# Four spans instead of three in the last output stage, and norm scales spread by a repeated stationary operand

## The chip, the cores and the metric

The kernel runs on one core of one Trainium2 chip. The metric is the device time of one execution in microseconds; the median of the runs counts. A core has five engines that work side by side, each through its own queue in order: TensorE (PE; its weight loads are listed apart as PEld), VectorE (DVE), ScalarE (ACT), GpSimd (POOL) and SyncE (SP, which here only issues DMAs). They wait for each other through semaphores.

## The reference

One inference step of a decoder trunk of two layers, for 1024 tokens of a prompt and 8 short sequences of 4 tokens: 1056 tokens of width 1024, all in fp32. Layer 0 is an RG-LRU block (causal convolution, gated linear recurrence), layer 1 an HGRN2 block (linear attention with gates and a matrix state). Cut to what matters here:

```python
def _rmsnorm(x, gain):
    xf = x.astype(jnp.float32)
    y = xf * lax.rsqrt(jnp.mean(xf * xf, axis=-1, keepdims=True) + EPS)
    return (y * gain.astype(jnp.float32)).astype(x.dtype)

def _hgrn_layer(x, g_norm, w_in, lb, o_gain, w_out, S0):
    xn = _rmsnorm(x, g_norm)
    ...
    y = (o.reshape(Bsz, T, INNER_B) * jax.nn.silu(gate)).astype(x.dtype)
    return x + y @ w_out, S_T.astype(x.dtype)

# _trunk: layer 0, layer 1, then
    return _rmsnorm(x, final_gain), jnp.stack(hs), jnp.stack(bufs), jnp.stack(Ss)
```

The outputs are the normalised tokens and the states of both layers. The change touches the end of layer 1, `x + y @ w_out` and the final norm, and the way in which every norm brings its scale to the data.

## The kernel before

**Layout.** Everything is kept transposed: the 1024 features of a token lie over 8 tiles of 128 partitions (`KD = 8`), the 1056 tokens (`TOK`) along the columns. A stage works on spans of tokens: three chunks of 352 columns (`CH`) in most stages, quarters of 264 in the products of layer 1.

**A product** in nearly full fp32 precision is three passes of the type fp32r (`mm3`, L262 to L264): each operand is split into a high and a low part, and high x high, high x low and low x high are added in one PSUM bank. Each of the three loads 128 stationary columns of weights and streams the tokens of the span. fp32 operands that are not split are used for small products; in the trace each of these shows as two passes.

**A norm** needs the sum of squares of each token, which lies over partitions. ScalarE squares the 8 tiles (`AF.Square`), VectorE or GpSimd adds the squares into one tile `acc`, and PE multiplies `acc` with a column of ones (`norm_sum`, L295 to L299): for every 128 tokens it yields a PSUM column whose partition is the token. ScalarE takes the root (L470, L1724), VectorE the reciprocal (L472, L1727), so that a tile `r` (`nr`) holds the scale of token 128*i + p in row p, column i. The scale must then lie along the columns and be the same in all partitions. For that, VectorE multiplies the unit matrix `ident` with each column of `r` into a row of diagonal matrices `dg` (L473 and L476; L1728 and L1732), and PE multiplies a tile of ones with it (L478, L1738): every partition of the result `bc` holds the scales of the span. In layer 0, `norm` (L460 to L479) does this six times, three times for the input and three times for the norm between the layers.

**The last output stage** begins when nearly all of `y @ w_out` is done: 5 of the 8 blocks of 128 features (`K1 = 5`) have been added to the residual `x2` before. The loop over `OUT` at L1761 takes the tokens in three spans of 512, 288 and 256. For each span it runs over the 8 output tiles `m`: 9 products (3 blocks by 3 passes) into a bank, an addition to the residual on VectorE (L1781), a square on ScalarE (L1783), and the square added on GpSimd (L1792). For the last span the squares of `m` from 4 on are not added but summed by PE directly, each as it comes, into one bank per 128 tokens. The span before is finished inside the next one: at `m = RM = 3` PE does its sums (`summed`) and the roots, at `m = SM = 6` its spread, followed by `finish` (L1747). `finish` scales the 8 tiles and sends them out: in the first span all 8 on VectorE (L1758, from PSUM); in later spans five there, and three by ScalarE (gain, L1755, possible earlier) and GpSimd (scale, L1756, from a copy of `bc` that ScalarE makes at L1751). The 8 output DMAs (recorded at L1759, issued by the helper at L332) alternate between the queues of SP and ScalarE. Behind the loop come two small products that keep PE busy (L1796), and the roots, spread and finishing of the last span.

**The order.** Within a layer the kernel does not issue instructions as it meets them: `fl.add` records each operation with its engine, an estimate of its duration, what it reads and writes and a priority, and at the end of the layer `fl.run` plans all of them (class `Flow`). The plan is a list schedule by priorities that are found from the far end backwards, followed by a random search over the operations of the first 60 us. PE operations marked `main=True` keep their order of recording; the others ("side") may go where the plan sees their inputs ready, with an extra distance `fl.side` from their producer (1.2 us by default, 0.4 in layer 1). The order of each engine is fixed by this before the kernel runs.

## Time and profile before

| | |
|---|---|
| median of 3 runs | 1031.57 us (1030.36 to 1032.78) |
| the profiled execution | 1031.86 us, of which the span of the profile is 1030.1 us |
| granted TensorE clock, mean | 0.997 of full speed |
| ACT, DVE and POOL busy in 981 to 998 us (first span) | 4.42, 5.39 and 7.03 us |
| the same in 1009.6 to 1019.4 us (third span) | 5.54, 8.52 and 4.88 us |
| output DMAs of 256, 144 and 128 KB, issue to landing | 1.7 to 2.6 us |

The span is what lies between the first and the last record; the time of a run has some more around it. A row of the timeline gives the start (us from the span's start), the time until the end, engine, line, operation, output and inputs, shapes, and the count where several like instructions follow each other (the duration is then that of all of them from the first start to the last end). A row of a group gives the line, engine, operation, shapes, the count, the busy time in us, the mean of one in ns, and the idle time before. A row of a stretch gives its bounds, its length and the busy us (with counts) of PE, PEld, DVE, ACT and POOL, then the granted clock, the share of the DMA engines and GB/s. Products are pipelined: a new one starts long before the record of the last ends, so that the pace of PE is read from start to start.

### The profile page before, as it was taken

To read this page: it belongs to the slowest core of one execution; us is meant where nothing else is said; L and a number is where in the kernel's file an instruction comes from. 1 tells how busy PE (TensorE), PEld (TensorE's weight loads), DVE (VectorE), ACT (ScalarE), POOL (GpSimd) and SP (SyncE) were. 2 spreads that over 40 slices of the span, in tenths; PEclk is the share of its full clock that TensorE was granted. 3 is DMA by queue.
4 is the path that set the end of the run, shared out by engine and by line. 5 is a ranking of instruction groups with operands and counts; after the bars stand their busy time and mean duration, and the time that the engine had idled before them with its cause. 6 is when DMAs were issued, how large, how long until landed. Compare 5 with 4: busy or idle time off the path is not lost.

```text
span 1030.1 us, 26451 instructions
## 1 busy us (share of the span) xinstructions
PE 1021.1 (99%) x10118; PEld 996.4 (97%) x10118; DVE 810.8 (79%) x1641; ACT 578.1 (56%) x1322; POOL 496.5 (48%) x569
## 2 busy tenths in 40 slices
PE   9999999999999999999999999999999999999997
PEld 9999999999999999999999999999999999999986
DVE  7999785867888699436599999798989799986436
ACT  8788747876775785335454463626363636552334
POOL 0117353544526236636425656555555557533544
PEclk9999999999999999999999999999999999999998
DMA  9201112112852487426474244343535353687204
GB/s 299 78 17 56 57 48 74 52 54 76 257 178 59 133 270 223 160 83 219 136 213 138 73 147 132 130 148 111 167 111 168 102 159 122 207 246 209 87 1 169
DMA packets 107854, 138.30 MB, mean 134 GB/s; under 512 B 23632, under 2 KB 85072, under 8 KB 107728
## 3 DMA queue, kind: packets, MB, share of 16 engines
q1 hardware_dynamic: 105424, 133.85, 42.1%
q10 hardware_dynamic: 2304, 2.77, 0.8%
q8 instruction: 79, 1.29, 0.5%
q14 instruction: 47, 0.39, 0.1%
HBM read 89.99 MB, written 41.61 MB: 128 GB/s over the span
## 4 chain that ended last, share of the span: by engine, by line
PE 93%; DVE 2%; DMA 2%; ACT 1%; issue 1%; POOL 1%; SPq 0%; POOLq 0%; DVEq 0%; ACTq 0%
PE mm L262 27%; PE mm L264 26%; PE mm L263 26%; PE hg L1085 2%; PE hg L592 1%; PE hg L262 1%; PE hg L264 1%; PE hg L263 1%; PE hg L753 1%; PE hg L1232 1%; PE hg L1287 1%; PE hg L1289 1%; DMA k<-yd 1%; PE mm L1085 0%; DMA vt<-sg 0%
## 5 line engine op out<-in xcount | busy, mean ns | idle before, releaser
L262 PE MATMUL mm<-xh,whi 128*128 128x352 f32 (+1 forms) x1127 | 352.6, 313 | 0.1
L264 PE MATMUL mm<-xh,wlo 128*128 128x352 f32 (+1 forms) x1127 | 348.1, 309 | 0.0
L263 PE MATMUL mm<-xl,whi 128*128 128x352 f32 (+1 forms) x1127 | 347.7, 309 | 0.0
L346 POOL TENSOR_TENSOR wlo<-wraw,whi 128x256 fp32r<-128x256 f32 (+3 forms) x188 | 200.8, 1084 | 199.7 <-ACT whi L403 97.3
L263 PEld LDWEIGHTS mm<-xl,whi 128*128 128x128 f32 x1127 | 212.5, 189 | 1.4 <-DVE xl L346 0.3
L262 PEld LDWEIGHTS mm<-xh,whi 128*128 128x128 f32 x1127 | 211.8, 188 | 2.1 <-DVE k L1545 0.3
L264 PEld LDWEIGHTS mm<-xh,wlo 128*128 128x128 f32 x1127 | 212.0, 188 | 0.0
L524 DVE SCALAR_TENSOR_TENSOR k<-xb,prm_sb,k 128x352 f32<-128x352 f32 (+2 forms) x144 | 82.3, 596 | 24.2 <-ACT k L521 20.7
L262 PE MATMUL mm<-t,whi 128*128 128x264 f32 (+1 forms) x330 | 96.6, 293 | 0.2 <-issue 0.2
L264 PE MATMUL mm<-t,wlo 128*128 128x264 f32 (+1 forms) x330 | 94.4, 286 | 0.0
L263 PE MATMUL mm<-t,whi 128*128 128x264 f32 (+1 forms) x330 | 94.4, 286 | 0.0
L1545 DVE TENSOR_TENSOR k<-mm,k 128x264 f32<-128x264 f32 x154 | 64.0, 424 | 11.7 <-PE mm L264 10.3
L346 POOL TENSOR_TENSOR wlo<-R,whi 128x256 fp32r<-128x256 f32 x70 | 58.3, 854 | 27.0 <-ACT whi L1469 24.1
L607 POOL TENSOR_TENSOR k<-X 128x352 f32<-128x352 f32 x36 | 43.6, 1217 | 52.8 <-DVE R L608 42.0
L1469 ACT CAST whi<-wraw 128x512 fp32r<-128x512 f32 x56 | 34.5, 618 | 60.4 <-DVE wraw L1479 26.0
L403 ACT CAST whi<-wraw 128x512 fp32r<-128x512 f32 (+2 forms) x79 | 44.3, 572 | 39.1 <-PE mm L263 28.9
L262 PEld LDWEIGHTS mm<-t,whi 128*128 128x128 f32 x330 | 62.1, 188 | 1.5 <-issue 0.3
L263 PEld LDWEIGHTS mm<-t,whi 128*128 128x128 f32 x330 | 62.2, 188 | 0.0
L264 PEld LDWEIGHTS mm<-t,wlo 128*128 128x128 f32 x330 | 62.1, 188 | 0.0
L262 PE MATMUL mm<-yh,whi 128*128 128x352 f32 x153 | 52.2, 341 | 0.0
L264 PE MATMUL mm<-yh,wlo 128*128 128x352 f32 x153 | 49.4, 323 | 0.0
L263 PE MATMUL mm<-yl,whi 128*128 128x352 f32 x153 | 49.4, 323 | 0.0
(458 smaller groups left out, 2513.9 us busy)
## 6 DMA issues: line engine op xcount, KB each, us to landing
wraw<-in_w_dram SPq DMA_DIRECT2D x88, 256.0 KB, 3.0
wraw<-in_wo_dram SPq DMA_DIRECT2D x34, 192.0 KB, 2.5
R<-in_w_dram SPq DMA_DIRECT2D x17, 256.0 KB, 3.9
si<-in_s_in_dram SPq DMA_DIRECT2D x8, 512.0 KB, 5.4
vt<-sg SPq DMA_DIRECT2D x8, 512.0 KB, 3.8
sg<-vt SPq DMA_DIRECT2D x32, 128.0 KB, 2.9
kt<-kt SPq DMA_DIRECT2D x8, 512.0 KB, 3.6
kt<-kt SPq DMA_DIRECT2D x32, 128.0 KB, 5.1
```

The lines of the kernel that those rows point to most:

```text
L262: T.matmul(out, wh, xh, start=first, stop=False)
L263: T.matmul(out, wh, xl, start=False, stop=False)
L264: T.matmul(out, wl, xh, start=False, stop=last)
L346: emit = lambda: e.tensor_tensor(b, x, a.bitcast(F32), op=ALU.subtract)
L403: act(m, lambda hi=hi, raw=raw, m=m: S.copy(hi[:, :m], raw[:, :m]), rk, (hk,), prio)
L524: dve(u, lambda src=src, dst=dst, sh=sh, k=k: V.scalar_tensor_tensor(dst, sh(src, k), pc("cw", 12 * k + m), dst, op0=ALU.mult, op1=ALU.add ...
L592: fl.add("PE", 0.62, lambda ps=ps, i=i, c=c: T.matmul(ps[:96, :CH], gs[:, i, :], ST[:96, chunk(c)], start=True, stop=True), (("gs",), *((" ...
L607: pool(CH, lambda x=x, a=a, b=b: G.tensor_tensor(x, a.bitcast(F32), b.bitcast(F32), op=ALU.add), (ak, bk), (xk,), 3)
L753: fl.add("PE", 0.25, lambda: T.matmul(warm[:, :128], ones, ones, start=True, stop=True), (), (wk,), 9)
L1085: T.matmul(ps[32 * j:32 * j + 32, n * w:n * w + w], B[:, o:o + 32], q(slice(o, o + 32)), start=True, stop=True, tile_position=(0, 32 * j))
L1469: act(512, lambda: S.copy(hi, raw), (rk,), (hk,), 2)
L1545: dve(QT, lambda: V.tensor_tensor(o[0], z[0], u[0], op=ALU.add), (z[1], u[1]), (o[1],), 0)
```

## The change

- `OUT` has four spans, of 448, 288, 192 and 128 tokens.
- The scales are spread without diagonal matrices. The new `spread_rows` multiplies, for each 128 tokens, column i of `r`, repeated 128 times as the stationary operand, with `ident`: row c of the unit matrix picks the scale of token c, and all 128 output partitions receive it. One fp32 product per 128 tokens takes the place of one product per span, and the VectorE operations that made `dg` go, in layer 1 and in the six norms of layer 0. There `dg` no longer takes a buffer of its ring.
- The sums and the spread of the span before are no longer `main` operations at `m = 3` and `m = 6`. They are recorded at `m = 0` as side operations and the plan places them, with `fl.side = 0.1` in this stage.
- In all spans but the last, the squares of `m = 6` and `m = 7` are added on VectorE instead of GpSimd.
- Estimates of the plan change with it (the spread's duration, the time that the output DMAs take), and `CUTS`, by which the residual's dependences are kept, follows the new spans.

```diff
--- before.py
+++ after.py
@@ -32,8 +32,7 @@
 SPOTS, SPOTS0, SPOTS1 = (-1, -1, 0, 2), (2, 5, -1, -1), (1, 5, 9, 13, 17, 20)
 K2 = 8 - K1
 NB4 = 6
-RM, SM = 3, 6
-OUT = ((0, 512), (512, 288), (800, 256))
+OUT = ((0, 448), (448, 288), (736, 192), (928, 128))
 
 D = 1024
 SEQ = 1024
@@ -298,6 +297,11 @@
         for s, (a, u) in zip(sums, spans(n)):
             T.matmul(s[:u], acc[:, a:a + u], ones[:, :1], start=start, stop=stop)
 
+    def spread_rows(bc, r, n):
+
+        for i, (a, u) in enumerate(spans(n)):
+            T.matmul(bc[:, a:a + u], r[:u, i:i + 1].to_broadcast([u, 128]), ident[:u, :u], start=True, stop=True)
+
     def new_acts():
         hs, ls = [], []
         for k in range(KD):
@@ -457,11 +461,10 @@
                 e = eng or G
                 (pool if e is G else dve)(CH, lambda: e.tensor_tensor(a[:, :CH], a[:, :CH], sq, op=ALU.add), (sk, ak), (ak,), 2)
 
-        def norm(acc, own=None, sums=None, sumk=()):
+        def norm(acc, sums=None, sumk=()):
 
             a, ak = acc
             r, rk = next(nrs)
-            dg, dk = own or next(xbs)
             if sums is None:
                 ps, pk = next(hg)
                 sums, sumk = [ps[:, i:i + 1] for i in range(4)], [pk]
@@ -470,12 +473,8 @@
                 act(4, lambda i=i, s=s, u=u: S.activation(r[:u, i:i + 1], s[:u], AF.Sqrt, bias=epsc[:u], scale=1.0 / D), sumk, (rk,), 0,
                     0.08)
             dve(4, lambda: V.reciprocal(r[:, :3], r[:, :3]), (rk,), (rk,), 0, True)
-            dve(256, lambda: V.tensor_tensor(dg[:, :256].rearrange("p (i n) -> p i n", i=2),
-                                             ident[:, None, :].to_broadcast([128, 2, 128]),
-                                             r[:, :2, None].to_broadcast([128, 2, 128]), op=ALU.mult), (rk,), (dk,), 0)
-            dve(96, lambda: V.tensor_scalar(dg[:, 256:CH], ident[:, :96], r[:, 2:3], None, op0=ALU.mult), (rk,), (dk,), 0)
             bc, bk = next(hg)
-            fl.add("PE", 0.7, lambda: T.matmul(bc[:, :CH], ones, dg[:, :CH], start=True, stop=True), (dk,), (bk,), 0)
+            fl.add("PE", 0.7, lambda: spread_rows(bc, r, CH), (rk,), (bk,), 0)
             return bc[:, :CH], bk
 
         def scaled_parts(c, k, x, xk, bc, bk, g, gk, e, prio=1):
@@ -894,7 +893,7 @@
                 squares(k, x, xk, accs[c], V, xos, (c, k) in MU)
             if c == 0:
                 dma(hct, hc, (), (("hct",),), 2, 196)
-            bc, bk = norm(accs[c], next(xrs))
+            bc, bk = norm(accs[c])
             if c == 0:
                 act(CH, lambda bc=bc: S.copy(bcs[0], bc), (bk,), (bcs[1],), 0)
             else:
@@ -1710,14 +1709,12 @@
                 key = ("spare", len(spare))
                 inherit(key, olds)
                 spare.append((o[:, a:a + 512], key))
-        accs, sqs, dgs, sb = cycle(spare[:2]), cycle(spare[2:5]), cycle(spare[5:7]), spare[7]
+        accs, sqs, sb = cycle(spare[:2]), cycle(spare[2:5]), spare[7]
         nr2 = cycle([(fixed(f"nr2{i}", [128, 4], F32, p1), ("nr2", i)) for i in range(2)])
 
         def roots(n, sums, ready):
 
             r, rk = next(nr2)
-            dg, dk = next(dgs)
-            f, u = n // 128, n % 128
             dve(4, lambda: V.memset(r, 1.0), (), (rk,), 0)
             srcs = [(slice(i, i + 1), s[:w]) for i, (s, (_, w)) in enumerate(zip(sums, spans(n)))]
             for q, src in srcs:
@@ -1725,23 +1722,18 @@
                     ready, (rk,), 0)
             w = len(srcs)
             dve(16, lambda: V.reciprocal(r[:, :w], r[:, :w]), (rk,), (rk,), 0)
-            dve(128 * f, lambda: V.tensor_tensor(dg[:, :128 * f].rearrange("p (i n) -> p i n", i=f),
-                                                 ident[:, None, :].to_broadcast([128, f, 128]),
-                                                 r[:, :f, None].to_broadcast([128, f, 128]), op=ALU.mult), (rk,), (dk,), 0)
-            if u:
-                dve(u, lambda: V.tensor_scalar(dg[:, 128 * f:n], ident[:, :u], r[:, f:f + 1], None, op0=ALU.mult), (rk,), (dk,), 0)
-            return dg[:, :n], dk
-
-        def spread(n, dg, dk, main):
+            return r, rk
+
+        def spread(n, r, rk, main):
 
             bc, bk = next(hg)
-            fl.add("PE", 0.002 * n, lambda: T.matmul(bc[:, :n], ones, dg, start=True, stop=True), (dk,), (bk,), 0, main=main)
+            fl.add("PE", 0.0023 * n, lambda: spread_rows(bc, r, n), (rk,), (bk,), 0, main=main)
             return bc[:, :n], bk
 
         def summed(acc, ak, n):
             s, sk = next(hg)
             sums = [s[:, i:i + 1] for i in range(4)]
-            fl.add("PE", 0.7, lambda: norm_sum(sums, acc, n, True, True), (ak,), (sk,), 0, main=True)
+            fl.add("PE", 0.7, lambda: norm_sum(sums, acc, n, True, True), (ak,), (sk,), 0)
             return roots(n, sums, (sk,))
 
         def finish(a, n, bc, bk):
@@ -1756,18 +1748,18 @@
                     pool(n, lambda x=x: G.tensor_tensor(x, x, sb[0][:, :n], op=ALU.mult), (sb[1], *xk), xk, 1)
                 else:
                     dve(n, lambda x=x, k=k: V.scalar_tensor_tensor(x, x, pc("gf", k), bc, op0=ALU.mult, op1=ALU.mult), (bk, *xk), xk, 1)
-                dma(yT[k][:, q], x, xk, (), 1, n / 2, S if k % 2 else Q)
-
+                dma(yT[k][:, q], x, xk, (), 1, 0.37 * n, S if k % 2 else Q)
+
+        fl.side = 0.1
         for a, n in OUT:
             q = slice(a, a + n)
             final = a + n == TOK
             cs = [c for c in range(NCH) if c * CH < a + n and (c + 1) * CH > a]
             acc, ak = next(accs)
             for m in range(KD):
-                if a and m == RM:
-                    dg = summed(*prev[:2], prev[3])
-                if a and m == SM:
-                    finish(*prev[2:], *spread(prev[3], *dg, True))
+                if a and m == 0:
+                    scales = summed(*prev[:2], prev[3])
+                    finish(*prev[2:], *spread(prev[3], *scales, False))
                 ps, pk = next(mm)
                 hi, lo, wk = late[m]
 
@@ -1788,6 +1780,8 @@
                         sums = [s[:, :1] for s, _ in sums]
                         fl.add("PE", 0.3, lambda acc=acc, n=n, sums=sums: norm_sum(sums, acc, n, True, False), (ak,), sumk, 0)
                     fl.add("PE", 0.3, lambda sq=sq, n=n, m=m, sums=sums: norm_sum(sums, sq, n, False, m == KD - 1), (sk, *sumk), sumk, 0)
+                elif m > 5:
+                    dve(n, lambda acc=acc, sq=sq, n=n: V.tensor_tensor(acc[:, :n], acc[:, :n], sq[:, :n], op=ALU.add), (sk, ak), (ak,), 1, True)
                 elif m:
                     pool(n, lambda acc=acc, sq=sq, n=n: G.tensor_tensor(acc[:, :n], acc[:, :n], sq[:, :n], op=ALU.add), (sk, ak), (ak,), 1)
             prev = acc, ak, a, n
```

## The prediction

> **What bounds the kernel now.** I read the busy shares first, then the chain that ended last, then the busy times of stretches.
>
> ```profile
> PE 1021.1 (99%) x10118; PEld 996.4 (97%) x10118; DVE 810.8 (79%) x1641; ACT 578.1 (56%) x1322; POOL 496.5 (48%) x569
> PE 93%; DVE 2%; DMA 2%; ACT 1%; issue 1%; POOL 1%; SPq 0%; POOLq 0%; DVEq 0%; ACTq 0%
> ...
> 30.00:60.00 30.00, 30.00 (x187) 29.58 (x186) 29.77 (x73) 20.74 (x49) 5.99 (x11) 1.00 0.15 44
> ...
> 1019.40:1023.70 4.30, 3.53 (x25) 2.85 (x25) 1.96 (x6) 2.29 (x7) 1.27 (x2) 1.00 0.70 240
> 1023.70:1030.10 6.40, 0.00 (x0) 0.00 (x0) 2.05 (x5) 0.35 (x1) 2.09 (x3) 0.50 0.50 165
> ```
>
> The reader is to see that TensorE (PE) works without a gap until 1019.4 us, even where VectorE (DVE) is as full as it is (29.77 of 30 us in the second stretch). Only behind 1019.4 does the kernel wait for something else. So a change is worth what it adds to or takes from PE's stream, plus what it does to the 10.7 us from the last product to the end of the span, 1030.1.
>
> **The stream of the output stage.** In the order of time, the starts of the three spans (72 products each: 8 rows by 9) and what interrupts them:
>
> ```profile
> 981.12 0.39 PE L262 MATMUL mm<-t,xh 128*128 128x512 f32 x1
> ...
> 997.78 0.29 PE L262 MATMUL mm<-t,xh 128*128 128x288 f32 x1
> ...
> 1001.41 0.95 PE L299 MATMUL mm<-ones,R 128*128 128x1 f32 x8
> 1002.22 0.38 PE L262 MATMUL mm<-t,xh 128*128 128x288 f32 x1
> ...
> 1007.61 0.30 PE L262 MATMUL mm<-t,xl 128*128 128x288 f32 x1
> ...
> 1009.59 0.28 PE L262 MATMUL mm<-t,xh 128*128 128x256 f32 x1
> ...
> 1012.77 0.65 PE L299 MATMUL hg<-ones,R 128*128 128x1 f32 x6
> ...
> 1019.11 0.28 PE L264 MATMUL mm<-t,xl 128*128 128x256 f32 x1
> 1019.23 0.50 PE L299 MATMUL hg<-ones,R 128*128 128x1 f32 x4
> ```
>
> First column start, second duration. The pace is start to start: at 512 columns (997.78-981.12)/72 = 0.2314 us, at 288 (1009.59-1007.61)/15 = 0.1320, at 256 (1012.77-1009.59)/27 = 0.1178. That is a line: 0.0044 a ten columns and 0.004 to begin with. On it 448 columns take 0.2030, 192 take 0.0894 and 128 take 0.0610. The three spans cost 72 x (0.2314+0.1320+0.1178) = 34.65 us. The stretch from 981.12 to 1019.23 is 38.11, so sums, spreads and their waits cost 3.46.
>
> **Narrow products: the load.** Each product loads its own 128 stationary columns. The groups of loads by shape, and one run of loads with almost nothing to multiply (one column each):
>
> ```profile
> L264 PEld LDWEIGHTS mm<-xh,wlo 128*128 128x128 f32 x1127 | 212.0, 188 | 0.0
> ...
> L1085 PEld LDWEIGHTS hg<-R,sg 128*32 128x32 f32 x768 | 9.2, 109 | 0.0
> L1170 PEld LDWEIGHTS hg<-R,sg 128*64 128x64 f32 x112 | 3.8, 137 | 0.3
> L1327 PEld LDWEIGHTS hg<-ident,kt 128*128 128x128 f32 x12 | 1.4, 141 | 0.0
> ...
> 1020.01 0.97 PEld L299 LDWEIGHTS hg<-ones,a 128*128 128x128 f32 x8
> ```
>
> The mean (last number) rises by 25 to 28 ns for 32 columns more, so a load of 188 ns is about 83 fixed and 105 of streaming. Eight in a row with only single columns behind them take 0.97, so one every (0.97-0.19)/7 = 0.111 us. Products of 256 columns or more (0.1178) hide that; no product of this type (fp32r) in the trace is narrower. At 192 and 128 columns the line falls under it, and I take the larger of the two: 0.111 for both. Bounds: 0.101, from the eight sums between 1001.41 and 1002.22, and 0.118, the pace at 256, below which nothing has been seen. Then the four spans cost 72 x (0.2030+0.1320+0.111+0.111) = 40.1 us, **5.5 more** than the three (from 4.0 to 6.5).
>
> The Trainium skill, "TensorE: Matmul & The Clock Gate", section "LDWEIGHTS (loading the stationary operand)", gives columns divided by 1.2 in ns, 107 for 128, which agrees with the 105 here. The same page, "Back-to-back issue gap", says that pairs of load and product sustain about 81 ns at 128 columns; by that figure the last span would cost 5.8 us and the sum below would come 2.2 lower, or 3.7 if 192 columns then ran on the line too. Its section "Weight-path perf modes — Fast Weight Load (FWL) and DoubleRow" keeps the faster load for types other than FP32; no row here shows which side fp32r falls on, except that its loads last as long as those of fp32.
>
> **Sums and spreads in the stream.** A spread was one fp32 product, which the trace shows as two passes; it becomes one product per 128 tokens, also two passes. The nearest rows, from the chain (start, duration, passes):
>
> ```profile
> 11.16 0.89 PE hg L753 x8
> ...
> 23.50 0.67 PE hg L753 x6
> ...
> 26.71 0.59 PE hg L478 x2
> ...
> 1006.25 1.12 PE L1738 MATMUL hg<-sg,ones 128*128 128x512 f32 x2 [0.22 <-DVE sg L1728]
> ```
>
> A 128-column fp32 pass costs 0.89/8 = 0.111. Repeating one column as the stationary operand is not in the trace; I price its load like any other of 128 columns, between nothing more (hidden as above) and double, 0.11 for each of some 27 products. In the stage behind the first spans there are 8+6+4 passes of sums and 8+6+4 of spreads: 36 x 0.111 = 4.0, and a switch between the two kinds of some 0.08 (the product at 1002.22 lasts 0.38 for 0.29) six times, so 4.4: **0.9 more** than 3.46 (from 0.5 to 1.1). Their fixed places go: PE works its queue in order, so a spread placed too early stops the products queued behind it, as the one at 1006.25 did for 0.2 to 0.4 us (it stands in the 3.46), while one placed late delays only the finishing of its span. I take no wait; one of that size for each of three spreads would add at most 1. In the first layer six spreads of 352 columns go from 0.59 to 0.67: **0.5 more**. The VectorE work removed there (two instructions a norm) lies beside a full PE and is worth nothing; PE has no wait to lose. The last two additions of squares of the first three spans go from POOL to VectorE, two each of about 0.6, 0.46 and 0.35 us, and 8 more output DMAs are issued at 0.34 us; both lie beside the products of the next span, and with four instead of three finishings VectorE still has under 4 us of work in the 8 us of the last span.
>
> **The tail.** The steps behind the last product:
>
> ```profile
> 1019.92 0.51 DVE L1758 SCALAR_TENSOR_TENSOR a<-a,prm_sb,mm 128x288 f32<-128x288 f32 x1
> 1020.34 0.42 DVE L1781 TENSOR_TENSOR sg<-mm,sg 128x256 f32<-128x256 f32 x1
> 1020.86 0.42 ACT L1783 ACTIVATE sg<-sg 128x256 f32<-128x256 f32 x1 [0.18 <-DVE sg L1781]
> 1021.33 0.61 PE L299 MATMUL hg<-ones,sg 128*128 128x1 f32 x4 [0.26 <-ACT sg L1783]
> 1021.75 0.48 ACT L1724 ACTIVATE nr<-hg,eps 128x1 f32<-128x1 f32 x2
> 1022.26 0.17 DVE L1727 RECIPROCAL nr<-nr 128x2 f32<-128x2 f32 x1 [1.50 <-ACT nr L1724]
> 1022.46 0.42 DVE L1728 TENSOR_TENSOR sg<-ident,nr 128x256 f32<-128x256 f32 x1
> 1022.94 0.70 PE L1738 MATMUL hg<-sg,ones 128*128 128x256 f32 x2 [0.46 <-DVE sg L1728]
> 1023.68 0.37 ACT L1751 COPY sg<-hg 128x256 f32<-128x256 f32 x1 [1.45 <-PE hg L1738]
> 1024.13 2.09 POOL L1756 TENSOR_TENSOR sg<-sg 128x256 f32<-128x256 f32 x3 [3.45 <-ACT sg L1751]
> 1024.98 0.34 ACTq L332 DMA_DIRECT2D out_yT_dram<-R  x1
> 1026.43 0.42 ACTq L332 DMA_DIRECT2D out_yT_dram<-sg  x1
> ...
> L1781 DVE TENSOR_TENSOR R<-mm,R 128x512 f32<-128x512 f32 x3 | 2.1, 692 | 4.2 <-PE mm L264 4.2
> L346 POOL TENSOR_TENSOR wlo<-wraw,whi 128x128 fp32r<-128x128 f32 x1 | 0.5, 452 | 0.0
> ```
>
> The last product ends at 1019.39, its add begins only at 1020.34: the engine still scales the span before (the row at 1019.92). With 128 columns, step by step: that 0.95 becomes 0.1, since in eight rows of 9 x 0.111 = 1.0 us each VectorE has an add of 0.29 and a few scalings to do (-0.8); the add goes from 0.42 to 0.29, by the 0.00106 a column between 692 at 512 and 422 here (-0.1); the square loses as much (-0.1); one root instead of two (-0.2); the diagonal and its gap go (-0.45); the spread's two passes shrink from 0.70 to 0.30+0.11 (-0.3); the copy (-0.1). Then ACT's four DMA issues: 1024.98 to 1026.43, 0.48 apart, so they are the limit rather than POOL, whose three multiplications fall from 2.09 to 3 x 0.45. The first can issue some 0.35 sooner (-0.35). From the last issue to the end 3.67 us pass; half the bytes take perhaps 0.5 less, at most 1 and at least nothing: I take -0.5. Sum **-2.9**, between -2.0 and -3.8.
>
> **The sum.** 5.5 + 0.9 + 0.5 - 2.9 = **+4.0 us**. The profiled execution took 1031.86 us (span 1030.1 and 1.8 around it), 0.3 above the median of the runs, 1031.57. On the median: **1035.5 us**. The whole order is planned anew from changed costs; what that can do I bound by the filler products (L753) that stand between real ones after 11 us, 0.89+0.67 and a few of 0.2, about 2 us: up to 1 either way. Own range of this case: 1033.3 to 1037.2.
>
> **Rivals.**
> - The load hides (chance 0.22). fp32r might load faster when pressed, as the loads of L1327 do for the same 128 columns: 141 ns, 49 less, which would put the floor at 0.111-0.049 = 0.062. Then both narrow spans run on the line, the four cost 34.95 (+0.3), and the result is 0.3+0.9+0.5-2.9 = -1.2: 1030.4 us, not slower. The sign turns where a 128-column pair takes less than about 0.078 us (with 192 on the line). For it: no row shows a narrow fp32r product. Against it: the 188 ns of its loads, and that L1327 transposes.
> - Half-way (0.08). Loads and products share the time, so that 128 columns go at the mean of line and floor, 0.086, and 192 on the line at 0.0894: +2.1 for the spans, +0.6 in all, 1032.2 us. The 81 ns that the Trainium skill states in the section on the issue gap, named above, lie near this case.
> - The floor holds but the tail keeps its queue (0.10): the new plan leaves scalings of the 192 span ahead of the last add and POOL's or ACT's part late, and the tail gains 1 instead of 2.9: 1037.5 us.
> - Narrow fp32r is worked like fp32 (0.04): two passes at half rate, 2 x 0.111 at 128 and 2 x 0.164 at 192, 72 x (0.222+0.328-0.222) = 23.6 more than the forecast: 1059 us. Nothing in the trace speaks for it but that all its widths are 256 or more.
>
> **Chances.** The forecast has 0.56. A measurement here can tell about 0.2% (2 us) from no change. Faster by more than that, below 1029.5: about half of the first rival, 0.10. Within it: the rest of that rival, most of the half-way one and the lowest corner of the forecast, 0.21. Slower: 0.69. The range, 1029.8 to 1037.5, takes in all but the lowest third of the first rival, the last one, half of the one before it and a tail of the forecast, about 0.2.
>
> **What would show it.** Paces start to start of 0.10 to 0.118 at both 192 and 128 columns, with loads back to back, show the floor; 0.09 and 0.06 show the first rival. The last span should last about 8 us instead of 4.4. Behind its last product: an add within 0.2, no L1728, one root, some 7.8 us to the end. The six first-layer spreads should be 0.67 long with the 128-column passes at 0.11; much longer ones would mean that the repeated column loads slowly. A span of the last stage whose products wait for VectorE, ScalarE or a bank would make the sum wrong in another place.

## The result, and the profile after

| | before | after |
|---|---|---|
| median of 7 runs each, same chip | 1031.57 us (1030.28 to 1033.72) | 1036.60 us (1035.30 to 1040.84) |
| ratio, after to before | | 1.0057 (95% interval 1.0037 to 1.0078) |
| profiled execution, its span, its mean clock | 1031.86, 1030.1, 0.997 | 1040.84, 1039.1, 0.993 |

The change makes the kernel 5.0 us slower; 1035.5 was forecast. The profiled execution of after is the longest of its seven, 4.2 above their median. The seven stand in two groups: three with a mean clock of 0.993 (1039.08 to 1040.84 us) and four with 0.997 or 0.998 (1035.30 to 1036.60). So this profile shows something that the median holds only in part, and it has to be found first.

The page of after, its busy shares and its chain by engine:

```profile
PE 1032.0 (99%) x10222; PEld 1010.9 (97%) x10222; DVE 805.4 (78%) x1646; ACT 584.6 (56%) x1337; POOL 488.2 (47%) x573
...
PE 91%; DVE 4%; ACT 2%; DMA 1%; issue 1%; SPq 0%; POOL 0%; DVEq 0%; POOLq 0%
```

PE is as full as before, and busy for 10.9 us more. The last stage of after, from the timeline of PE and its loads (start, duration, count behind the x):

```profile
982.20 0.36 PE L261 MATMUL mm<-t,xh 128*128 128x448 f32 x1
...
996.82 0.29 PE L261 MATMUL mm<-t,xh 128*128 128x288 f32 x1
...
1006.16 1.19 PE L303 MATMUL hg<-ident,nr 128*128 128x128 f32 x8
1007.28 0.40 PE L261 MATMUL mm<-t,xl 128*128 128x288 f32 x1
...
1008.56 0.25 PE L261 MATMUL mm<-t,xh 128*128 128x192 f32 x1
...
1016.58 0.68 PE L298 MATMUL hg<-ones,R 128*128 128x1 f32 x6
...
1017.46 0.27 PE L263 MATMUL mm<-t,xh 128*128 128x128 f32 x1
...
1020.14 0.27 PE L263 MATMUL mm<-t,xh 128*128 128x128 f32 x1
1020.25 0.99 PE L303 MATMUL hg<-ident,nr 128*128 128x128 f32 x6
1021.17 0.33 PE L261 MATMUL mm<-t,xh 128*128 128x128 f32 x1
...
1024.43 0.42 PE L261 MATMUL mm<-t,xl 128*128 128x128 f32 x1
1024.64 0.42 PE L262 MATMUL mm<-t,xl 128*128 128x128 f32 x1
...
1026.99 1.35 PE L303 MATMUL mm<-ident,nr 128*128 128x128 f32 x4
...
1030.04 0.41 PE L263 MATMUL mm<-t,xl 128*128 128x128 f32 x1
```

Read from start to start, the paces are 0.2031 us at 448 columns ((996.82-982.20)/72), 0.1114 at 192 ((1016.58-1008.56)/72, with nothing between) and 0.1117 at 128 ((1020.14-1017.46)/24). Then, at 1024.43, the pace of the same products goes from 0.11 to 0.21 from one to the next. The busy times of stretches of after say why (bounds, length, busy us and counts of PE, PEld, DVE, ACT, POOL, then the granted clock):

```profile
1008.50:1016.60 8.10, 8.10 (x75) 8.10 (x73) 7.16 (x17) 3.88 (x10) 2.99 (x5) 1.00 0.46 171
1016.60:1024.40 7.80, 7.80 (x69) 7.58 (x68) 4.47 (x16) 3.59 (x14) 3.46 (x6) 1.00 0.33 115
1024.40:1030.20 5.80, 5.80 (x27) 5.46 (x27) 1.83 (x5) 1.89 (x6) 1.14 (x3) 0.50 0.38 130
```

The clock falls to half at 1024.4 with PE busy all the time: 7.80 of 7.80 us ahead of it and 5.80 of 5.80 behind. Before, it halved only where PE had run out of work (the stretch from 1023.7 in the prediction). From 1024.4 to the end are 14.7 us, and half the clock in 14.7 of 1039.1 us is a mean of 0.993: the lower mean of this group of runs is just this stretch.

The spans of the two profiles differ by 9.0 us. Their parts, each from rows above, from the prediction's, or from the run "e6_full_rows" below, which shows the tail and the side work of the same spans with the clock full until the last product:

| part | before | after | difference |
|---|---|---|---|
| start of the stage | 981.12 | 982.20 | +1.1 |
| products of the spans, at full clock | 34.5 | 40.1 | +5.6 |
| sums and spreads between them, at full clock | 3.46 | 5.1 | +1.6 |
| start of the last product to the end, last product at full clock | 10.99 | 8.19 | -2.8 |
| half clock from 1024.43 on | | | +3.6 |

The last row: some 21 products at 0.213 instead of 0.1115 (+2.1), the spread of 1026.99 at half pace (+0.6), and the tail 9.06 instead of 8.19 (+0.9). The parts add up to 9.1. Two more traces bear them out: those of "e4_paces" and "e7_shares" below end with the stage of the change and keep the full clock past its last product. There it is 45.29 and 45.27 us from the first product to the last, 5.2 more than the 40.08 of the products, and 8.22 and 8.55 us from there to the end.

Of the start of the stage nothing can be said for the change: in the profiles of seven of the kernels below it lay between 979.37 and 982.50, and 979.37 is that of the very same kernel ("e5_again").

### The profile page after: what moved, and what is told of

Read it like the earlier page. It is cut to its first block, busy times and chain, and to the rows that moved or that the text cites. A ratio compares the mean times of both kernels' runs of the same rounds, so it can differ in the third digit from the quotient of the medians.

```text
span 1039.1 us, 26704 instructions
## 1 busy us (share of the span) xinstructions
PE 1032.0 (99%) x10222; PEld 1010.9 (97%) x10222; DVE 805.4 (78%) x1646; ACT 584.6 (56%) x1337; POOL 488.2 (47%) x573
## 4 chain that ended last, share of the span: by engine, by line
PE 91%; DVE 4%; ACT 2%; DMA 1%; issue 1%; SPq 0%; POOL 0%; DVEq 0%; POOLq 0%
PE mm L261 26%; PE mm L262 25%; PE mm L263 25%; PE hg L591 1%; PE hg L1084 1%; PE hg L261 1%; PE hg L263 1%; PE hg L262 1%; PE hg L1286 1%; PE hg L752 1%; PE hg L1288 1%; PE hg L1231 1%; DMA sg<-xn 1%; DMA a<-on 1%; PE hg L303 1%
## 5 line engine op out<-in xcount | busy, mean ns | idle before, releaser
L1468 ACT CAST whi<-wraw 128x512 fp32r<-128x512 f32 x56 | 34.5, 619 | 61.9 <-DVE wraw L1478 31.9
```

Source lines behind the costliest of these rows:

```text
L1468: act(512, lambda: S.copy(hi, raw), (rk,), (hk,), 2)
```

## The experiments

Three questions: which part of the change costs the time; whether the floor of the narrow products is their load; what the two things are that the sum had not, the dearer spreads and the half clock.

### Which part

**e1_spans_only** is the kernel before with the new spans alone.

```diff
-OUT = ((0, 512), (512, 288), (800, 256))
+OUT = ((0, 448), (448, 288), (736, 192), (928, 128))
```

> The kernel before with nothing changed but the four spans 448, 288, 192 and 128; the scales are still spread through diagonal matrices and the sums and spreads stand at their fixed places. Theory (load floor): 72 products each at 0.203, 0.132, 0.111 and 0.111 us are 40.1 us against 34.65, +5.5; one more set of sums and a spread, +0.5; a tail shorter by about 2.4 (it keeps a diagonal of 128): about 1035.2 us, with the products 0.111 apart at both 192 and 128 columns. Rival (the cost is in the new spread and the plan): the spans by themselves gain, about 1029.5 us. If narrow products also make the clock halve, as in the profiled run of the change, some runs show a mean granted clock of 0.993 and take some 4 us more, about 1039.

Measured: 1036.59 us (1034.80 to 1037.79, 5 runs) beside 1032.21 of the kernel before, ratio 1.0037 (1.0024 to 1.0050). The spans alone bring 4.4 us, about all of the loss. Its timeline of PE has the same floor, and the old spread of 192 tokens:

```profile
1015.80 0.27 PE L262 MATMUL mm<-t,xh 128*128 128x128 f32 x1
...
1018.37 0.27 PE L264 MATMUL mm<-t,xh 128*128 128x128 f32 x1
...
1022.01 0.54 PE L1738 MATMUL hg<-sg,ones 128*128 128x192 f32 x2
1022.26 0.36 PE L262 MATMUL mm<-t,xl 128*128 128x128 f32 x1
```

23 paces in 2.57 us are 0.1117. The old spread holds the products up for 0.25 us (1022.01 to 1022.26). From the last product, at 1024.24, to the end at 1033.0 it is 8.8 us: 2.2 less than with a last span of 256. The rest of the tail's gain, 0.6, would be that of the spread without diagonal; the plan differs too, so this is not shown.

**e2_wide_spans** is the other half: the change with the spans of before.

```diff
-OUT = ((0, 448), (448, 288), (736, 192), (928, 128))
+OUT = ((0, 512), (512, 288), (800, 256))
```

> The change with the three spans of before (512, 288, 256): only the new spread, the plan's placing and the additions on VectorE stay. Load floor: no product is under it; the first layer's six spreads cost 0.5 more, the tail loses its diagonal (-0.45) and perhaps some of its queue: 1031.6 us within 1, granted clock 0.997 in all runs. Rival (the new spread and the plan cost the time): about 1035.6 us.

Measured: 1032.47 us (11 runs), ratio 0.9999 (0.9990 to 1.0008). The new spread and the free placing cost nothing that can be measured where the spans are wide. Its timeline of PE shows that the plan used its freedom otherwise than the old fixed places:

```profile
1017.99 0.28 PE L263 MATMUL mm<-t,xl 128*128 128x256 f32 x1
...
1018.92 1.02 PE L303 MATMUL hg<-ident,nr 128*128 128x128 f32 x6
```

The spread of the second span now stands behind the last product. That product starts 37.07 us after the stage does (980.92) instead of 37.99, and from it to the end, 1030.4, it is 12.4 us instead of 11.0: work went from the stream to the tail, and nothing was won.

**e10_four_wide** keeps four spans and makes none narrow.

```diff
-OUT = ((0, 448), (448, 288), (736, 192), (928, 128))
+OUT = ((0, 288), (288, 256), (544, 256), (800, 256))
```

> The change with four spans that are all wide: 288, 256, 256 and 256. Load floor: 72 x (0.132 + 3 x 0.118) = 35.0 us of products, only 0.3 over three spans; one more set of sums and spread, 0.5; the first layer 0.5; a tail shorter by the diagonal and part of its queue, 0.45 to 1: about 0.5 us over before, within 1 of it, clock never below 0.995. Rival (the number of spans, with its sums, spreads and finishings, makes the change slow): about as slow as the change, 4 us over before.

Measured: 1031.96 us (11 runs) beside 1032.20, ratio 0.9999 (0.9990 to 1.0007). So it isn't the number of spans, with one more set of sums, spreads and output DMAs, that costs the time. It is that two of them are narrow.

### Load or width

**e4_paces** puts series of products like those of the stage ahead of it, into a bank that nobody reads. It was executed once.

```diff
+        for cols, wide, times in ((128, 256, 60), (128, 224, 60), (128, 192, 120), (128, 256, 60), (128, 128, 120), (128, 256, 60),
+                                  (64, 128, 120), (128, 256, 60)):
...
+                T.matmul(probe[:cols, :wide], whi[:, :cols], yh[K1][:, :wide], start=True, stop=True) for _ in range(times)],
```

> The change with series of products of one weight block added ahead of the output stage, whose results are not used: 60 of 256 columns, 60 of 224, 120 of 192, 60 of 256, 120 of 128, 60 of 256, 120 of 128 columns with only 64 stationary columns loaded, 60 of 256. Load floor: 0.118 us each at 256, 0.111 to 0.112 at 224, 192 and 128 with 128 loaded columns; about 0.06 (the line) at 128 columns with 64 loaded ones, since the load halves. Rival (a fixed price of narrow products): 0.111 with 64 loaded columns too. Rival (the stream): 0.104, 0.089 and 0.061. The clock: if narrow products halve it, the series of 128 (13 us) shows a granted clock of 0.5 after some us and twice the pace, the series of 256 behind it brings it back, and the series of 192, whose array is busier, may or may not show it.

The groups of the series (shape of the stationary operand, of the streamed one, count, then busy us):

```profile
L1758 PE MATMUL mm<-t,xh 128*128 128x256 f32 x240 | 29.2, 282 | 0.0
L1758 PE MATMUL mm<-t,xh 128*128 128x192 f32 x120 | 13.6, 275 | 0.0
L1758 PE MATMUL mm<-t,xh 128*128 128x128 f32 x120 | 13.5, 274 | 0.0
L1758 PE MATMUL mm<-t,xh 128*64 128x128 f32 x120 | 7.4, 223 | 0.0
L1758 PE MATMUL mm<-t,xh 128*128 128x224 f32 x60 | 6.8, 274 | 0.0
```

Busy time by count: 0.122 us at 256, 0.113 at 224 and 192, 0.1125 at 128 columns, each with a little of the neighbours in it. With 128 columns streamed and only 64 loaded it is 0.062, which is the 0.061 that the prediction's line has for 128. So streaming 128 columns takes 0.061 us, and it is the load of 128 columns that makes 0.111 of it. The Trainium skill, "TensorE: Matmul & The Clock Gate", section "LDWEIGHTS (loading the stationary operand)", gives the loaded columns divided by 1.2 in ns, 107 for 128 columns; the measured 0.111 agrees to 4%. The 81 ns of the same page's "Back-to-back issue gap" is not reached at 128 columns of this type.

**e3_padded** tests the same in the kernel: the products of the narrow spans stream 256 columns, of which the addition reads the last 192 or 128 only.

```diff
+                u = max(n, 256)
+                v = slice(a + n - u, a + n)
...
-                        mm3(ps[:, :n], (hi[:, w], lo[:, w]), yh[K1 + k][:, q], yl[K1 + k][:, q], k == 0, k == K2 - 1)
+                        mm3(ps[:, :u], (hi[:, w], lo[:, w]), yh[K1 + k][:, v], yl[K1 + k][:, v], k == 0, k == K2 - 1)
...
-                dve(n, lambda x=x, ps=ps, n=n: V.tensor_tensor(x, ps[:, :n], x, op=ALU.add), (pk, *xk), xk, 0)
+                dve(n, lambda x=x, ps=ps, n=n, u=u: V.tensor_tensor(x, ps[:, u - n:u], x, op=ALU.add), (pk, *xk), xk, 0)
```

> The change, but the products of the spans of 192 and 128 tokens stream 256 columns (the tokens ahead of the span are multiplied again and not used). Load floor: a 256-column product takes 0.118 us where a 128-column one takes 0.111, so 144 products cost only 1.0 us more although they stream 33% and 100% more columns: 1036.7 us. If the half clock at the end comes from narrow products that leave the array idle part of the time, no run shows a clock of 0.993 and none is over 1038, so that the slowest runs of the change (1039 to 1041) are beaten. Rival (the stream sets the pace of narrow products): 72 x (0.118-0.089) + 72 x (0.118-0.061) = 6.2 us more, about 1042. Rival for the clock (chance, or the end of the kernel): about three runs in seven still show 0.993 and 4 us more.

Measured: 1036.55 us (1035.85 to 1037.19, 5 runs), ratio 1.0038 (1.0025 to 1.0050), mean clock 0.998 or 0.999 in all five. A third more columns in one span and twice as many in the other, and the time is not told apart from that of the change. The stretch of its last span that answers to the halved one of after:

```profile
1020.00:1026.20 6.20, 6.20 (x53) 5.98 (x51) 4.00 (x12) 2.52 (x9) 3.01 (x6) 1.00 0.50 168
```

The clock stays full. In the stream the wider products do cost what the paces say (144 times 0.1178-0.1115, 0.9 us): from the first product of the stage to the last it is 46.18 us, against the 45.3 of the change at full clock. What they would save is the half clock, which the change meets in some executions only.

### The spreads

**e5_again** is the change once more, beside which the next one was run.

> The change itself once more, for the share of its runs in which the clock halves early and as the base of the next one. If narrow products bring the halving: again some of the runs at a mean granted clock of 0.993 to 0.995 and some 3 us or more over the others, which the padded version did not show in any of five. If that was chance: all at 0.996 or above and within 2 us of each other.

Measured: 1036.91 us (1036.30 to 1038.31, 5 runs), ratio 1.0043 (1.0029 to 1.0057). Its longest run, 1038.31, has the mean clock 0.993 and is the one with the profile; the others have 0.996 or 0.997. It is 1.7 us over their median, 1036.6, and not the 3 that was expected. So the clock halved early in 4 of the 12 executions of the change, two of them seen in a profile and two told by their mean clock.

**The rows of a spread.** In after, the last of the four products of the first spread has only 64 rows (448 is 3 x 128 + 64). The loads of this spread and the next product, from the timeline of after:

```profile
1006.60 0.19 PEld L303 LDWEIGHTS hg<-ident,nr 128*128 128x128 f32 x1
...
1006.91 0.18 PEld L303 LDWEIGHTS hg<-ident,nr 64*128 64x128 f32 x1
...
1007.27 0.19 PEld L261 LDWEIGHTS mm<-t,xl 128*128 128x128 f32 x1
```

The load of 64 rows begins 0.31 us after the last one of 128; loads that follow each other in the stream begin 0.11 apart. Behind the two passes of 64 rows, the first full load comes 0.36 after the first of them, where two paces would be 0.22. **e6_full_rows** gives the short pieces all 128 rows; the rows added meet columns of the unit matrix that are zero there.

```diff
-            T.matmul(bc[:, a:a + u], r[:u, i:i + 1].to_broadcast([u, 128]), ident[:u, :u], start=True, stop=True)
+            T.matmul(bc[:, a:a + u], r[:, i:i + 1].to_broadcast([128, 128]), ident[:, :u], start=True, stop=True)
```

> The change with one difference: each piece of a spread uses all 128 rows of the scales and of the unit matrix, also where it yields only 64 or 32 columns. In the profile of the change the two passes of a 64-row or 32-row piece take about 0.35 us more than two passes of a 128-row piece: the load begins 0.31 after the last one instead of 0.11, and the next product 0.25 after it. Theory (a change of the rows in use empties the array): spreads of 448 columns take 0.9 instead of 1.12 us, of 288 0.67 instead of 0.92, the last stage is about 1.0 us shorter, and the time 1.0 below the change. Rival (the repeated column loads slowly, whatever the rows): no difference in the spreads.

Measured: 1035.52 us (1035.18 to 1035.76, 6 runs), ratio 1.0032 (1.0021 to 1.0043); 1.4 below the change that was run beside it, and 1.1 below those four of its executions that kept the clock. A seventh execution took 5708.64 us, for a reason that the record doesn't show, and is left out. Its timeline, the three spreads, the last product and what follows that:

```profile
1004.89 1.00 PE L303 MATMUL hg<-ident,nr 128*128 128x128 f32 x8
1005.70 0.38 PE L261 MATMUL mm<-t,xl 128*128 128x288 f32 x1
...
1018.66 0.80 PE L303 MATMUL hg<-ident,nr 128*128 128x128 f32 x6
1019.30 0.31 PE L261 MATMUL mm<-t,xh 128*128 128x128 f32 x1
...
1025.21 0.27 PE L263 MATMUL mm<-t,xl 128*128 128x128 f32 x1
...
1025.70 0.28 DVE L1773 TENSOR_TENSOR sg<-mm,sg 128x128 f32<-128x128 f32 x1
...
1026.86 0.39 ACTq L336 DMA_DIRECT2D out_yT_dram<-sg  x1
...
1027.30 0.26 ACT L1721 ACTIVATE nr<-hg,eps 128x1 f32<-128x1 f32 x1 [0.48 <-POOL sg L1748]
...
1029.27 0.34 ACTq L336 DMA_DIRECT2D out_yT_dram<-R  x1
...
1030.70 0.40 ACTq L336 DMA_DIRECT2D out_yT_dram<-sg  x1
```

The spread of 448 holds the products up for 0.81 us instead of 1.12, that of 288 for 0.64 instead of 0.92 (1020.25 to 1021.17 in after). With the same at the third, 0.9 us go, though the products now work on more rows; from the first product of the stage to the last it is 44.27 us, 1.0 less than the 45.3 of the change at full clock. The change of rows was the cost, not the work. The Trainium skill, "TensorEngine Tiling (Array Packing)", section "Key Properties", states that a change of the tiling mode drains TensorE, without a price. The trace agrees, if pieces of 64 and of 32 rows are such a change, with 0.3 us for the two switches around a piece. In layer 0, whose short pieces have 96 rows, the six passes of a spread take 0.58 to 0.64 us in after (0.64 from 28.12 to 28.76); in e6_full_rows, with 128 rows, five of the six take as long. So nothing that shows is added there.

**e9_wide_full** puts the full rows on the wide spans of before.

```diff
-OUT = ((0, 448), (448, 288), (736, 192), (928, 128))
+OUT = ((0, 512), (512, 288), (800, 256))
...
-            T.matmul(bc[:, a:a + u], r[:u, i:i + 1].to_broadcast([u, 128]), ident[:u, :u], start=True, stop=True)
+            T.matmul(bc[:, a:a + u], r[:, i:i + 1].to_broadcast([128, 128]), ident[:, :u], start=True, stop=True)
```

> The change with the three spans of before and full rows in every spread: nothing narrow and no change of rows is left, only the spread without diagonals and the plan's placing. Against the same three spans without full rows (0.9999 of before) one spread gets 0.3 us shorter: 0.9996 of before, 1031.4 where before is 1031.8, within 1 us of it; not to be told from no change. If the new spread were worth what its saved diagonals add up to in the tail (0.45) and nothing else cost anything: up to 1 us faster.

Measured: 1032.26 us (11 runs) beside 1032.20, ratio 1.0003 (0.9994 to 1.0012). There only one piece is short, of 32 rows, and the plan puts it behind the last product anyway. No version was found that beats the kernel before.

### The clock

**e7_shares** asks whether the clock halves by how little PE streams, though it never waits. Series of 112, 96, 64 and 32 columns, each with its load of 128, stand between series of 256. It was executed once.

```diff
+        for cols, wide, times in ((128, 256, 60), (128, 112, 120), (128, 256, 60), (128, 96, 120), (128, 256, 60), (128, 64, 120),
+                                  (128, 256, 60), (128, 32, 120), (128, 256, 60)):
```

> Series of 120 products of 112, 96, 64 and 32 columns, each with its own load of 128 stationary columns, between series of 60 of 256 columns, ahead of the output stage of the change; their results are not used. At 0.111 us a product the array streams 42, 36, 24 and 12% of the time (48% at 128, where 13 us in the earlier series left the clock at full speed), and TensorE never waits. Theory (the clock halves where the array streams too small a share of some window): the granted clock is 0.5 in part of one of these series, certainly at 32, and the pace there is 0.21; the 256 series restores it. Rival (only waiting halves it): full clock in all, 0.111 us a product throughout.

The stretches of 112, of 256, of 96 in two parts (the second with the first of the 256 behind it), and of the 256 behind them:

```profile
987.00:1000.40 13.40, 13.40 (x122) 13.40 (x121) 0.00 (x0) 0.00 (x0) 0.00 (x0) 1.00 0.01 1
1000.40:1007.50 7.10, 7.10 (x63) 7.10 (x62) 0.00 (x0) 0.00 (x0) 0.00 (x0) 1.00 0.00 0
1007.50:1014.30 6.80, 6.80 (x64) 6.80 (x62) 0.00 (x0) 0.00 (x0) 0.00 (x0) 1.00 0.01 2
1014.30:1029.00 14.70, 14.70 (x72) 14.70 (x71) 0.00 (x0) 0.00 (x0) 0.00 (x0) 0.50 0.00 0
1029.00:1036.50 7.50, 7.50 (x55) 7.50 (x55) 0.00 (x0) 0.00 (x0) 0.00 (x0) 0.84 0.01 2
1036.50:1041.00 4.50, 4.50 (x43) 4.50 (x41) 0.00 (x0) 0.00 (x0) 0.00 (x0) 1.00 0.00 0
```

112 columns run at full clock to the end of their 13.3 us (988.13 to 1001.47). The first product of 96 columns starts at 1008.64, so that 1.1 us of the third stretch still belong to 256. At the same pace and with PE and its loads busy throughout, the products of 96 lose the full clock at 1014.35, after 5.7 us, and wider products bring it back; those of 64 and 32 lose it too. In these series it is the share of the time in which columns are streamed that decides. By the prediction's 0.00044 us a column, 112 columns stream for 0.050 of 0.111 us, 45%, and 96 for 38% (42 and 36% in the expectation, which counts 0.00042 a column). The last span of after, from 1017.2 to 1024.4, had 51 products of 128 (51 x 0.057, 2.9 of 7.2 us, 40%), the rest of it sums, which stream one column, the spread of 288 and its drains. That is an estimate, and it leaves out what the spread's few passes stream; it lies near the two that were measured, which would fit with a clock that halves in some executions and not in others.

The clock's own records in the traces say more. The clock changes only at steps of 3.41 us: from its first fall on, e7_shares has 17.07 us at half, 10.24 at full, 20.48 at half and 10.24 at full clock, which are 5, 3, 6 and 3 steps, and the full clock ahead of the fall lasts 1017.17 us in after and in e5_again, 298 steps. The steps lie otherwise against the program in each execution: the full clock begins 7.24 us into the span in after, 4.13 in e5_again. In the last step ahead of the fall after has 24 products of 128 and four sums, 40% by the same count, and e5_again 22 and four, with two short passes, 38%. The step of e6_full_rows that lies as after's does has 26 and four, 43%, and keeps the clock. But e4_paces, whose last stage is that of the change, keeps it over a step with 36% (1087.33 to 1090.74: 19 products, four passes of a spread, four sums). So counting columns is not the whole rule in this stage, and what the passes of a spread count for stays open.

The Trainium skill, "TensorE: Matmul & The Clock Gate", section "What's actually happening", ties the clock to how busy PE has been of late; the runs agree, with the addition that a PE which is busy with loads counts as partly idle.

That the sums and drains in the last span are what tips the change over wasn't varied alone. The early halving was seen in 4 of 12 executions of the change, in none of the 5 with 256 columns streamed, none of the 5 of e1_spans_only and none of the 6 of e6_full_rows. Each of these alone could be chance, and they differ from the change in different things; together they speak for it without showing it.

### A wider last span

**e8_wide_best** was to be the best version: full rows and a last span of 240, just under the width that covers the load.

```diff
-OUT = ((0, 448), (448, 288), (736, 192), (928, 128))
+OUT = ((0, 512), (512, 304), (816, 240))
...
-            T.matmul(bc[:, a:a + u], r[:u, i:i + 1].to_broadcast([u, 128]), ident[:u, :u], start=True, stop=True)
+            T.matmul(bc[:, a:a + u], r[:, i:i + 1].to_broadcast([128, 128]), ident[:, :u], start=True, stop=True)
```

> A version without narrow products: the new spread with full rows and the plan's placing, but three spans of 512, 304 and 240 tokens, 240 being where a product by the line (0.0042 + 0.000444 a column) takes the 0.111 us of a load. Spans 34.7 us as before; spreads 0.1 less than before; tail shorter by the diagonal (0.45) and some 0.2 for 16 columns fewer; the first layer 0.5 more: 0.3 us faster than before, within 1, so hardly to be told from it. If the floor were lower than 0.111 at 240, up to 0.4 better.

Measured: 1037.34 us (5 runs), ratio 1.0050 (1.0037 to 1.0062): 5.6 us above the kernel before, where 0.3 below it was expected. These spans have pieces of 48 and 112 tokens, and part of the prompt's output comes out wrong with them, for a reason that is not known, so the time is read for the order of the work alone. From the start of the last stage to the end it is 49.6 us (49.0 before), but that start is late, at 986.04 us. Its waits of PE (who waited for whom: us, times, longest) and a stretch of layer 1:

```profile
PE mm L261 <- DVE k L1544: 2.1, 2, 1.8
...
520.00:700.00 180.00, 178.21 (x2707) 173.13 (x2706) 161.82 (x346) 87.36 (x223) 98.57 (x113) 0.99 0.42 129
```

Hundreds of us ahead of the last stage PE waits 1.8 us in one place for VectorE, and the clock falls with it (0.99): half clock from 592.30 to 595.71, which costs another 1.7 us. In e2_wide_spans PE is busy for all 180 us of that stretch. The plan of layer 1 has presumably come out otherwise; the two orders were not compared. The waits and the half clock are 3.8 of the 5.6 us; where the rest arose stays open, all the more as the start varies by itself. So this run says little of spans of 240; it suggests that an edit in the last stage can move the work ahead of it too.

## Why the prediction held, step by step

- **What bounds the kernel, the floor, and the spans: right.** PE is not quite without gaps ahead of 1019.4 (979.39 us busy of the first 981, and 0.22 idle at 1006), but nothing of the sum hangs on that. The pace was taken as 0.111 us at both narrow widths and measured as 0.1114 and 0.1117; the products cost 5.6 more where 5.5 was forecast. e4_paces shows the reason that was given, the load.
- **Sums and spreads: the term that was mis-sized.** Forecast +0.9 (0.5 to 1.1), measured +1.6 at full clock. Priced were 36 passes at 0.111 and a switch between two kinds of 0.08; not priced was that a piece of 64 or 32 rows costs some 0.3 us by the two switches of rows around it. Three such pieces make 0.9. Without them, in e6_full_rows, the stream has 4.2 us beside its products (44.27 from 980.94 to the last product, less 40.08), where the prediction's 36 passes and switches came to 4.4. The repeated column, which had been left open between nothing and twice the load, costs like any other of 128: passes of 0.81/8 = 0.10.
- **Layer 0: +0.5 forecast, none seen, and the row was misread.** The 0.59 of the old spread is a step of the chain, which runs on to the end of the last pass; from start to start, the old spread holds the products up for 0.32 us (0.33 once) and the new one for 0.58 to 0.64. That is 1.6 for six, three times the forecast. Yet layer 0 does not get longer: from its first product of 352 columns to the product behind its last spread it is 485.03 us before (9.47 to 494.50) and 484.97 after (9.81 to 494.78); in e1_spans_only, with the old spread, it is 485.5. What makes up for the 1.6 was not looked into. PE's wait for VectorE at the start of the kernel, 1.0 us, is there in both.
- **The tail: -2.8 for -2.9, by luck, with two sizes off that cancel.** From the start of the last product to the first of ACT's last four issues it is 4.06 us in e6_full_rows and 5.87 before, 1.8 less where 2.4 had been taken; from the last issue to the end 2.7 instead of 3.67, 1.0 less where 0.5 had been taken. Add 0.2 behind the last product, one root, no diagonal, as said. Part of the shortfall is the root: it begins 0.86 us after the last sum (1026.44), and ACT does no work in the last 0.48 of them, as it issues an output DMA of the span before (the row at 1026.86).
- **The new plan: within the 1 us allowed** as far as the change goes; e8_wide_best shows that the bound was narrow, with a stage that starts 3.5 us behind the latest of the others (986.04 and 982.50).
- **Not in the prediction: the half clock** ahead of the end, +3.6 us in the profile of after, and met in a third of the executions. It moves the median by less: the eight of the change's twelve without it have a median of 1036.3.
- **The rivals.** That the load hides, and the half-way case, fell with 0.111 and with the 0.062 that is reached only when 64 columns are loaded. Products at fp32's rate fell with the same rows. The tail that keeps its queue came true in the root alone.

5.6 + 1.6 - 2.8 = +4.4 without the half clock, against +4.0 forecast. The medians differ by 5.0, and by 4.7 (1036.3 to 1031.6) where the clock did not halve early. That the forecast came so near owes something to luck: 0.7 too little for the spreads stood against 0.5 too much for layer 0.

## What to carry to other kernels

A last span cut narrow shortens what stands behind the last product, but only down to the width at which a product still covers the load of its stationary operand; below that every column taken away is time spent on loads, here 72 times 0.05 us for 128 columns, and the tail has to give back more than that. Ahead of such a cut, work out the pace from load and width and the share of the time that PE streams. Where a matrix product takes a short piece among full ones, fill it up with zero rows if the rows are there anyway.

## What the runs showed of the hardware that had not been expected

- The clock can halve with PE busy and nothing waiting: 96 columns every 0.111 us for 5.7 us are too little, 112 are enough for 13.3 us and longer was not tried. At half clock the loads slow down as well (0.213 us a pair). It changes at steps of 3.41 us only, which lie otherwise in each execution.
- A piece of 64 or 32 rows among pieces of 128 costs 0.3 us by the two switches, one of 96 rows nothing that shows.
- The start of the last stage differs by 2.8 us between two profiles of the same kernel (979.37 and 982.20), so a stage's start from one profile is no proof of an effect ahead of it.
